# A hybrid decoder block on one core: the chunked scan spread over the projection steps, and the last attention head and last output parts in ascending order

## The chip, the core and the metric

The kernel runs on one NeuronCore of a Trainium2 chip. The metric is the device time of one execution in microseconds (us); the time of a kernel is the median over its runs. The engines are TensorE (PE, with its weight loads shown apart as PEld), VectorE (DVE), ScalarE (ACT), GpSimd (POOL) and SyncE (SP), which issues nearly all DMAs of this kernel in order from one queue.

## What is computed

One layer, 2048 tokens of width 1024, float32. The input is RMS-normalised and goes through one projection `w_in`, whose columns belong to three parallel branches; their outputs are joined to 2048 columns and go through one projection `w_out`:

```python
u = rms_norm(h, norm_g)
proj = einsum('bsd,de->bse', u, w_in)
q, k, v, z_att, f_raw, z_ssd, xbc, dt_raw, x_lru, z_lru = split(proj)
y_att = fox_attention(q, k, v, log_f, ...) * silu(z_att)     # 8 heads x 64, causal
y_ssd = ssd_mixer(xbc, dt_raw, z_ssd, ...)                   # 16 heads x 64, 2 groups, chunks of 128
y_lru = rglru_mixer(x_lru, ...) * silu(z_lru)                # 512 channels
h = h + einsum('bse,ed->bsd', concat([y_att, y_ssd, y_lru]), w_out)
```

The chunked scan (`ssd_mixer`) works for each chunk `c` of 128 tokens and each group `g` of 8 heads: a product C·B, weighted with the causal decay, times `x·dt` (the diagonal part); C times the carried state; and the new state, which is the old one decayed plus B times `x·dt·decay`. Its result is gated and its sum of squares kept for a group norm.

## The kernel before

All products are done in float32 split into a high and a low part (`float32r`, names ending in `h` and `l`), so that one projection is three products: high·high, high·low, low·high. The program is traced in Python; a scheduler then orders each engine's instructions from its own estimate of times, by priority (program order, unless a block raises it with `high_priority`), and adds the semaphores. Each engine runs its list in order. `issue_after(ins)` puts the instructions of a block that run on the engine of `ins` behind it.

The work comes in these stages, in the order of the program:

1. Norm and transposition of the input to `uh`, `ul` (four blocks of 512 tokens), projections of x/B/C with their convolution (`pxx`), the gates, v of heads 0 to 3, the LRU branch with its projections (`pll`, `pzl`) and the scan's gate z (`group_zs`, `pzs`), up to about 754 us. Intermediate results go to DRAM tensors (`xs_d`, `b_d`, `bt_d`, `ct_d`, `zs_d`, `acs_d`).
2. The scan: 16 chunks by 2 groups, 32 units of `ssd_unit`. A unit loads its tiles, makes `cb` (L675), twice loads a row of cumulated decays broadcast to all partitions into `ab` (L686), masks it on POOL (L689), takes exponentials on ScalarE (L693), multiplies by `cb` (L694) and makes four heads of `py` (L698). Then `po` from the state (L705), `pn` for the new one (L715), and the transposed result goes to `gt_d` (store, one unit late). The tile `ab` has two buffers.
3. Attention projections, traced behind the scan but with no dependence on it: for each head pair `p` eight calls of `proj_tok2` (`pqk`, L343 to L347), after p = 1 eight calls for v (`group_v`), after p = 2 and p = 3 eight calls each of `proj_ch` for the gate `z_att` (`group_za`, `pza`): 56 calls. Since the scan was traced first, the scheduler lets these calls fill in around it. After p = 2, `load_head(0)` and `load_q(0)` are traced. They load keys, values and queries of head 0 into tiles that lie where the scan's tiles lay.
4. Attention: `units` are (head, block of 256 queries), 64 of them, with `sb + 1` tasks each, 288 in all. `ORD` gives the order of the blocks: head 0 from block 7 down to 0, heads 1 to 6 up, head 7 down. Each task makes scores (`T`), two exponentials, and three tasks later the product with v (`O`); the row maxima for the next unit (`S`, L970) are spread over the tasks. `finish` closes a unit and calls `later(store, 1)`.
5. The output projection is a generator, `sweeps`, of 512 steps of three products (L1145 to L1147) each: 256 for the parts of LRU and scan group 1, then 256 for scan group 0 and attention (`work`). Four steps make a half of 512 columns in one PSUM bank, which VectorE then adds to `xr` or `xo` (L1151, L1153). During attention the pool `psP` has one bank; after it `psP2` has six. `fill` takes a number of steps after each attention task:

```python
want = FIRST + count[0] * RATE // 288 + MORE * max(0, count[0] - 288 + END)
```

A part of attention can be taken only when the head-7 unit that covers its tokens has been finished (`ready`); for that the row sums of all eight heads are read back from DRAM, inverted and written again (L1098 to L1100). `later(f, n)` runs `f` when the task counter has advanced by `n`. `work` runs through the tokens from the last tile to the first:

```python
work = [(NT - 1 - t, i) for t, i in work]
```

`anchor[1]` is the last product of the fifth of the last eight `pza` calls; the row maxima of the first attention unit and the first 12 output steps are put behind it.

## Time and profile before

| | us |
|---|---|
| median of 3 runs (2012.23 to 2016.85) | 2012.35 |
| profiled execution | 2011.36 |
| its span, first to last instruction | 2009.5 |
| TensorE busy | 1946.7 (97%) |
| TensorE weight loads busy | 1705.1 (85%) |
| VectorE busy | 1296.2 (65%) |
| ScalarE busy | 1005.0 (50%) |
| POOL busy | 807.9 (40%) |

The profiled execution is one run, on the slowest core; 1.86 us of its time lie outside the span. Busy times are shares over all stages. Matmuls are pipelined, so that the mean duration of one (400 ns for 512 columns) is longer than the distance from one to the next; what a product costs in a stream is read from a window, busy time by the number of records. The granted clock of TensorE is given as a share of 2.4 GHz; 0.50 is 1.2 GHz.

### The profile page before, as it was taken

What the parts mean: (1) busy time and instruction counts of PE and PEld (TensorE: products, weight loads), DVE (VectorE), ACT (ScalarE), POOL (GpSimd) and SP (SyncE); (2) the same over time, 40 slices, a digit from 0 to 9 for tenths busy, and PEclk for the clock granted to TensorE, in tenths of its full rate; (3) what the DMA queues carried; (4) which work ended last, traced back from release to release, by engine and by line L of the source; (5) the groups of instructions that cost most, each with busy time, mean ns of one, the idle gap of its engine ahead of it and who ended that gap; (6) DMA issues with size and microseconds to landing.
All of it is one profiled execution on the core that took longest, in us unless ns stands there. A gap on an engine that the chain in (4) does not pass through costs nothing.

```text
span 2009.5 us, 34885 instructions
## 1 busy us (share of the span) xinstructions
PE 1946.7 (97%) x11941; PEld 1705.1 (85%) x11941; DVE 1296.2 (65%) x2573; ACT 1005.0 (50%) x2174; POOL 807.9 (40%) x920
## 2 busy tenths in 40 slices
PE   7999999999999999899999999999999999998899
PEld 6898888898989899787888897888899888887787
DVE  6748555573645556767667534788788887896333
ACT  7625444453544544444444333576777776675010
POOL 0100000232222224445555200687888887786110
PEclk9999999999999999999999999999999999999999
DMA  5332223121212135657666724765565764523353
GB/s 191 84 100 67 70 74 105 48 65 43 70 38 75 32 114 140 185 169 209 206 198 175 197 81 141 217 166 156 164 169 163 196 161 143 173 83 113 123 173 126
DMA packets 260032, 261.30 MB, mean 130 GB/s; under 512 B 26724, under 2 KB 198016, under 8 KB 258304
## 3 DMA queue, kind: packets, MB, share of 16 engines
q1 hardware_dynamic: 259696, 259.05, 43.7%
q8 instruction: 95, 1.56, 0.3%
q0 software_dynamic: 160, 0.03, 0.1%
q14 instruction: 81, 0.66, 0.1%
HBM read 164.22 MB, written 94.77 MB: 129 GB/s over the span
## 4 chain that ended last, share of the span: by engine, by line
PE 44%; DMA 3%; DVE 2%; issue 1%; ACT 1%; POOL 1%; SPq 1%; DVEq 0%; POOLq 0%; ACTq 0%
PE po L1145 6%; PE po L1146 5%; PE po L1147 5%; PE T L1011 3%; PE T L1012 3%; PE O L1067 3%; PE O L1069 3%; PE S L970 3%; PE pza L360 1%; PE pza L361 1%; PE pza L359 1%; PE pqk L345 1%; PE pqk L343 1%; PE pqk L347 1%; DMA ab<-acs_d 1%
## 5 line engine op out<-in xcount | busy, mean ns | idle before, releaser
L1145 PE MATMUL po<-woh,mh 128*128 128x512 f32 x512 | 204.9, 400 | 13.9 <-DVE xo L1151 11.4
L1024 DVE TENSOR_TENSOR pl<-T,ph 128x512 fp32r<-128x512 f32 (+1 forms) x288 | 185.5, 652 | 38.9 <-ACT T L1023 32.7
L1146 PE MATMUL po<-wol,mh 128*128 128x512 f32 x512 | 202.4, 395 | 0.0
L1147 PE MATMUL po<-woh,ml 128*128 128x512 f32 x512 | 201.7, 395 | 0.0
L1022 ACT ACTIVATE ph<-T 128x512 fp32r<-128x512 f32 (+1 forms) x288 | 165.4, 574 | 51.0 <-PE T L1012 43.5
L1037 POOL TENSOR_TENSOR ac<-ac,ph 128x512 f32<-128x512 f32 x120 | 158.7, 1323 | 23.8 <-ACT ph L1022 18.1
L1023 ACT ACTIVATE T<-T 128x512 f32<-128x512 f32 (+1 forms) x288 | 164.7, 572 | 0.3
L359 PE MATMUL pxx<-uh,wh 128*128 128x512 f32 x384 | 152.8, 400 | 1.1 <-ACT uh L304 1.0
L360 PE MATMUL pxx<-ul,wh 128*128 128x512 f32 x384 | 153.1, 400 | 0.0
L361 PE MATMUL pxx<-uh,wl 128*128 128x512 f32 x384 | 150.9, 395 | 0.0
L347 PE MATMUL pqk<-wh,ul 128*128 128x256 f32 x512 | 150.9, 295 | 0.0
L980 DVE TENSOR_REDUCE mc<-S 128x1 f32<-128x512 f32 x192 | 128.5, 682 | 32.4 <-PE S L970 30.7
L1067 PE MATMUL O<-ph,vv 128*128 128x256 f32 (+1 forms) x576 | 148.1, 278 | 0.6 <-ACT ph L1022 0.5
L1011 PE MATMUL T<-q,k 128*128 128x256 f32 x576 | 146.3, 279 | 2.1 <-ACT q L995 1.6
L345 PE MATMUL pqk<-wl,uh 128*128 128x256 f32 x512 | 148.3, 290 | 0.0
L343 PE MATMUL pqk<-wh,uh 128*128 128x256 f32 x512 | 147.8, 289 | 0.0
L420 DVE SCALAR_TENSOR_TENSOR accx<-rtx,cv,accx 128x512 f32<-128x512 f32 x144 | 108.3, 753 | 57.7 <-ACT accx L417 54.7
L345 PE MATMUL pzs<-wl,uh 128*128 128x256 f32 x512 | 143.6, 281 | 0.0
L347 PE MATMUL pzs<-wh,ul 128*128 128x256 f32 x512 | 143.3, 281 | 0.0
L343 PE MATMUL pzs<-wh,uh 128*128 128x256 f32 x512 | 143.0, 281 | 0.0
L1012 PE MATMUL T<-qx,kx 128*128 128x256 f32 x576 | 142.7, 279 | 0.0
L1069 PE MATMUL O<-pl,vv 128*65 128x256 f32 x576 | 141.4, 277 | 0.0
(357 smaller groups left out, 5693.2 us busy)
## 6 DMA issues: line engine op xcount, KB each, us to landing
ab<-acs_d SPq DMA_DIRECT2D x64, 256.0 KB
pt_d<-xr SPq DMA_DIRECT2D x64, 256.0 KB
wr<-in_w_in_dram SPq DMA_DIRECT2D x112, 128.0 KB
xt<-in_x_dram SPq DMA_DIRECT2D x16, 512.0 KB
xs_d<-stx SPq DMA_DIRECT2D x32, 256.0 KB
v_d<-vs SPq DMA_DIRECT2D x32, 256.0 KB
wr<-in_w_in_dram SPq DMA_DIRECT2D x128, 64.0 KB
zs_d<-zs SPq DMA_DIRECT2D x32, 256.0 KB
```

The lines of the kernel that those rows point to most:

```text
L343: T.matmul(ps[:, i, :], h[k][:, sl], wh[k], start=(k == 0 and i == 0), stop=False, skip_group_check=True)
L345: T.matmul(ps[:, i, :], h[k][:, sl], wl[k], start=False, stop=False, skip_group_check=True)
L347: ins = T.matmul(ps[:, i, :], l[k][:, sl], wh[k], start=False, stop=last, skip_group_check=True)
L360: T.matmul(ps, wh[k][:, ms], ul[tb][k], start=False, stop=False)
L1011: T.matmul(ps, k2[:, ks], q3[:, qs], start=(jj == 0), stop=False, skip_group_check=True)
L1012: ins = T.matmul(ps, kx[:, ks], qx[:, qs], start=False, stop=True, skip_group_check=True)
L1024: marks["V"].append(V.tensor_tensor(pl[:, 0:n], pt[:, 0:n], ph[:, 0:n].bitcast(F32), op=ALU.subtract))
L1067: T.matmul(po[:, qs], vv[:, kt, 0:128], ph[:, cs], start=(kt == 0), stop=(kt == 2 * sb + 1), skip_group_check=True)
L1069: T.matmul(po[0:65, q2], vv[:, kt, 64:129], pl[:, cs], start=False, stop=False, skip_group_check=True)
L1145: T.matmul(ps, mh[:, j, :], h, start=(j == 0), stop=False)
L1146: T.matmul(ps, mh[:, j, :], l, start=False, stop=False)
L1147: T.matmul(ps, ml[:, j, :], h, start=False, stop=(j == 3))
```

## The change

The scan becomes a generator, `ssd_steps`. A unit yields after its loads, `cb` and the two `ab`; after `po`; after each half of `py`; and at its end: five times, 160 in all, with a last step for the closing norm. The calls of the attention projections now tick after every second `k`, four times a call. `scan` counts the ticks and takes scan steps such that 160 steps fall on `SPAN` = 184 of the 224 ticks. Each step is traced at raised priority, its TensorE instructions behind the projection product of the tick. `ab` gets a pool of four buffers. The store of a unit's result is split: transposition and copy at the end of the next unit, its DMA in the unit after that. While ticks run, the weights of the projections are traced at raised priority too. When the scan has ended, `begin` closes its pools, opens those of attention and loads head 0; this was traced after the scan and after p = 2 before.

Head 7 takes its blocks from 0 up to 7, `work` runs through the tokens from the first tile on, the term with `MORE` and `END` is removed from `fill`, and read-back, reciprocal and write of the row sums are called 2, 4 and 5 tasks after the unit's stores, its `ready` after 8. `run_late` takes the entries in the order of their due times.

```diff
-END = 14
-MORE = 2
-ORD = (DOWN,) + (UP,) * 6 + (DOWN,)
+ORD = (DOWN,) + (UP,) * 7
+SPAN = 184
...
+    def tick(ins):
+        if between[0] is not None:
+            between[0](ins)
...
+        if between[0] is not None:
+            with tc.high_priority(offset=HP):
+                return split_weights(cols, rawp, eng, i, n)
+        return split_weights(cols, rawp, eng, i, n)
...
+            if k % 2:
+                tick(ins)
...
+    s4 = sx.enter_context(tpool(name="s4", bufs=4, side="right"))
-    def ssd_unit(c, g):
+    def ssd_unit(c, g, before):
...
-        py = psY.tile([P, 512], F32, name=f"py{u}", tag="Y")
+        abs_ = []
         for q in range(2):
-            ab = s2.tile([P, 4, P], F32, name=f"ab{u}_{q}", tag="ab")
+            ab = s4.tile([P, 4, P], F32, name=f"ab{u}_{q}", tag="ab")
...
-            for e in range(4):
-                o = (q * 4 + e) * 64
-                T.matmul(py[:, o:o + 64], ab[:, e, :], xd[:, q * 4 + e, :], start=True, stop=True)
...
+            abs_.append(ab)
+        yield
+        last[1]()
         if state[g] is not None:
             po = psY.tile([P, 512], F32, name=f"po{u}", tag="Y")
...
+        yield
+        py = psY.tile([P, 512], F32, name=f"py{u}", tag="Y")
+        for q, ab in enumerate(abs_):
+            for e in range(4):
+                o = (q * 4 + e) * 64
+                T.matmul(py[:, o:o + 64], ab[:, e, :], xd[:, q * 4 + e, :], start=True, stop=True)
+            yield
...
+        before()
...
-            dma(gt_d[g][:, :, tsl].rearrange("i p t -> p i t"), yt)
...
+            last[1] = lambda: dma(gt_d[g][:, :, tsl].rearrange("i p t -> p i t"), yt)
+
+        last[0] = store
+
+    def ssd_steps():
+        for c in range(NT):
+            for g in range(2):
+                yield from ssd_unit(c, g, last[0])
+                yield
+        last[1]()
+        last[0]()
+        last[1]()
...
+    def begin():
...
+        make_k2(0)
+        load_head(0)
+        load_q(0)
...
+        def scan(ins):
+            done[0] += 1
+            while done[1] >= 0 and done[1] * SPAN < done[0] * 160:
+                done[1] += 1
+                with tc.high_priority(offset=HP), tc.issue_after(ins.ins):
+                    if next(ssd, 0) == 0:
+                        done[1] = -1
+                if done[1] < 0:
+                    begin()
+
+        between[0] = scan
...
-            if p == 2:
-                load_head(0)
-                load_q(0)
+        between[0] = None
...
-            dma(sr, s_d[qt].rearrange("i h t -> (i h) t"))
-            V.reciprocal(sr, sr)
-            dma(r_d[qt].rearrange("i h t -> (i h) t"), sr)
-            later(lambda: ready.add(sb), 4)
+            later(lambda: dma(sr, s_d[qt].rearrange("i h t -> (i h) t")), 2)
+            later(lambda: V.reciprocal(sr, sr), 4)
+            later(lambda: dma(r_d[qt].rearrange("i h t -> (i h) t"), sr), 5)
+            later(lambda: ready.add(sb), 8)
...
-        while late and (t is None or late[0][0] <= t):
-            late.pop(0)[1]()
+        while True:
+            due = [z for z in late if t is None or z[0] <= t]
+            if not due:
+                return
+            due = min(due, key=lambda z: z[0])
+            late.remove(due)
+            due[1]()
...
-        work = [(NT - 1 - t, i) for t, i in work]
...
-        want = FIRST + count[0] * RATE // 288 + MORE * max(0, count[0] - 288 + END)
+        want = FIRST + count[0] * RATE // 288
```

## Rows read from the trace of the kernel before

**Rows 1.** Cores: span of each and mean granted clock of TensorE.

```profile
core 0: 2009.5 us, clock 0.993
```

**Rows 2.** Windows by stage: us, busy us (instructions) of five engines, granted clock, DMA share, GB/s.

```profile
754.00:1123.00 369.00, 345.34 (x2487) 304.71 (x2486) 254.31 (x430) 171.67 (x483) 179.52 (x181) 0.98 0.62 181
...
1253.00:1300.00 47.00, 43.98 (x242) 37.01 (x240) 32.52 (x71) 23.04 (x48) 30.23 (x27) 0.96 0.77 217
1300.00:1800.00 500.00, 495.06 (x3268) 444.34 (x3267) 417.72 (x989) 365.44 (x836) 408.46 (x453) 1.00 0.55 157
1800.00:1850.00 50.00, 44.01 (x288) 39.31 (x287) 35.90 (x84) 32.83 (x76) 36.51 (x43) 1.00 0.40 119
1850.00:1900.00 50.00, 40.75 (x159) 31.52 (x159) 17.34 (x37) 4.76 (x9) 6.65 (x8) 0.90 0.38 118
1900.00:2000.00 100.00, 100.00 (x443) 82.81 (x442) 41.46 (x94) 11.20 (x18) 10.34 (x8) 1.00 0.49 156
2000.00:2009.50 9.50, 5.68 (x26) 4.36 (x24) 2.26 (x6) 0.00 (x0) 0.00 (x0) 0.92 0.25 96
```

**Rows 3.** Windows, finer, around the end of attention; columns as above.

```profile
1750.00:1800.00 50.00, 49.10 (x315) 42.78 (x315) 46.78 (x98) 35.57 (x79) 40.70 (x38) 1.00 0.29 99
...
1850.00:1855.00 5.00, 2.18 (x12) 1.52 (x11) 1.33 (x3) 1.04 (x3) 2.08 (x4) 0.94 0.61 189
1855.00:1860.00 5.00, 3.73 (x9) 2.99 (x10) 2.42 (x5) 0.00 (x0) 0.72 (x1) 0.50 0.19 56
```

**Rows 4.** Waits of TensorE, 750 to 1130 us: sum, times, longest us.

```profile
PE py L698 <- DVE ab L694: 6.7, 6, 1.9
PE py L698 <- issue: 3.1, 3, 1.5
PE py L698 <- POOL xs L701: 2.6, 1, 2.6
```

**Rows 5.** Chain that ended last, in the scan: start, us, what.

```profile
1088.28 4.58 DMA ab<-acs_d
1092.98 0.65 POOL ab L689
1093.65 1.29 ACT ab L693 x4
1095.02 0.70 DVE ab L694
1095.76 1.24 PE py L698 x8
```

**Rows 6.** Waits of the DMA queue SP, 750 to 1260 us.

```profile
SPq L686 <- PE py L698: 50.8, 34, 3.1
```

**Rows 7.** Waits of TensorE, 1800 to 1900 us.

```profile
PE po L1145 <- DVE xo L1151: 11.4, 5, 3.7
```

**Rows 8.** Waits of VectorE, 1780 to 1900 us.

```profile
DVE sr L1099 <- DMA sr<-s_d: 10.3, 4, 4.5
```

**Rows 9.** Windows of `pqk` alone: us, TensorE busy (records), clock, DMA share, GB/s.

```profile
1150.00:1200.00 50.00, 40.10 (x332) 1.00 0.32 92
```

**Rows 10.** Windows of `pza` alone; columns as in the group above.

```profile
1200.00:1250.00 50.00, 42.46 (x179) 1.00 0.43 140
```

**Rows 11.** Timeline of SP: start us, us of issue, instruction.

```profile
1136.78 0.46 SPq L805 DMA_DIRECT2D k<-kh_d  x1
...
1148.41 0.46 SPq L822 DMA_DIRECT2D qx<-ql_d  x1
...
1233.42 15.90 SPq L405 DMA_DIRECT2D za_d<-zt  x4
```

**Rows 12.** Timeline of POOL; in brackets idle time before and its releaser.

```profile
1136.99 0.52 POOL L778 MEMSET q<- 64x512 f32 x1 [7.44 <-DMA gt_d<-yt]
```

**Rows 13.** Line L698: records, duration ns, first and last start us.

```profile
L698 PE MATMUL py<-xd,ab x512: 217/275/446, 762.3 to 1123.2; 128*128 128x64 f32 x171
```

**Rows 14.** Line L970; columns as above.

```profile
L970 PEld LDWEIGHTS S<-k,q x320: 186/188/286, 1235.6 to 1826.4; 96*128 96x128 f32 x160
```

More of the change, by code (lines that the diff above doesn't have):

```diff
@@ L178, in hybrid_block @@
                    for k in range(KD)])
+    anchor = [None, None]
+    between = [None]
+    def tick(ins):
+        if between[0] is not None:
+            between[0](ins)
     gcount = [0]
@@ L361, in proj_ch @@
             ins = T.matmul(ps, wl[k][:, ms], uh[tb][k], start=False, stop=(k == KD - 1))
+            if k % 2:
+                tick(ins)
         anchor[0] = ins
@@ L783, in hybrid_block @@
-    for i in range(2):
-        make_q(kc)
-    k2s = {}
-    def make_k2(b):
-        k2 = (kvB if b else kvA).tile([P, S], F32R, name=f"k2{b}")
-        G.memset(k2[64:128, :].bitcast(F32), 0.0)
-        G.memset(k2[96:97, :].bitcast(F32), -1.0)
-        k2s[b] = k2
-    make_k2(0)
+    kp_ = {}
     heads = {}
     qs_ = {}
+    q3s, qxs = [], []
+    k2s = {}
     def load_head(h):
@@ L823, in load_q, with make_q, make_k2 @@
         qs_[j // 2] = q3, qx
+    kc = kvA = kvB = zm = onr = idr = zmt = None
+    def make_q(pool):
+        i = len(q3s)
+        q3 = pool.tile([P, 512], F32R, name=f"q3{i}")
+        G.memset(q3[64:128, :].bitcast(F32), 0.0)
+        G.memset(q3[64:66, :].bitcast(F32), 1.0)
+        q3s.append(q3)
+        qxs.append(pool.tile([P, 512], F32R, name=f"qx{i}"))
+    def make_k2(b):
+        k2 = (kvB if b else kvA).tile([P, S], F32R, name=f"k2{b}")
+        G.memset(k2[64:128, :].bitcast(F32), 0.0)
+        G.memset(k2[96:97, :].bitcast(F32), -1.0)
+        k2s[b] = k2
+    def begin():
+        nonlocal kc, kvA, zm, onr, idr, zmt
+        sx.close()
+        sgx.close()
+        kc = cx.enter_context(tpool(name="kc", bufs=1, side="right"))
+        kvA = cx.enter_context(tpool(name="kvA", bufs=1, side="right"))
+        zm = kc.tile([P, 640], F32, name="zm")
+        G.memset(zm, 0.0)
+        G.affine_select(out=zm[:, 512:640], in_=zm[:, 512:640], pattern=[[-1, P]],
+                        compare_op=ALU.is_ge, fill=-NEG, base=0, channel_multiplier=1)
+        onr = kc.tile([P, 65], F32R, name="onr")
+        G.memset(onr[:, 0:64].bitcast(F32), 0.0)
+        G.memset(onr[:, 64:65].bitcast(F32), 1.0)
+        idr = kc.tile([P, P], F32R, name="idr")
+        V.tensor_copy(idr, ident)
+        zmt = kc.tile([P, P], F32R, name="zmt")
+        V.tensor_scalar(zmt, tri, NEG, -NEG, op0=ALU.mult, op1=ALU.add)
+        for i in range(2):
+            make_q(kc)
+        make_k2(0)
+        load_head(0)
+        load_q(0)
     def load_wo(ws, k0, half, last, behind=()):
```

56 lines of the change are left out of this document (14 added, 42 removed).

## The prediction

> **What bounds the kernel now.** I read the span first [rows 1], then the span cut into stages [rows 2]. The reader is to see that TensorE is the bound from end to end: in the output stretch 1900 to 2000 us it is busy all 100 us, in the attention loop 1300 to 1800 it sits idle 500 − 495.06 = 4.94 us, 1%. No other engine comes near; the busiest, VectorE, has 417.72 of 500 there. So the time can only shrink where TensorE is idle or runs below its full clock, and the stages show two such places.
>
> The first is 754 to 1123 us, where the scan runs beside the q/k projections: 369 − 345.34 = 23.7 us idle, and a granted clock of 0.98 where the loop and the output stretch have 1.00. The second is the end of attention, 1800 to 1900: 5.99 + 9.25 = 15.2 us idle, and 0.90 of the clock in its second half, as the 5 us from 1855 at 0.50 show [rows 3]: the lower of the two levels, 1.2 GHz. In the 5 us ahead of that the engine had been busy for 2.18 only.
>
> Then the waits inside these places. In the scan TensorE waits before the diagonal product `py` (L698): 6.7 us for the multiplied decay tile `ab` (L694), 3.1 us where the profile names no releaser, 2.6 us for POOL [rows 4]. The chain shows why: decay row by DMA 4.58, mask 0.65, four exponentials 1.29, product with `cb` 0.70, then `py` 1.24 [rows 5]: 8.5 us in a row, and the DMA can only start when a buffer of `ab` is free. There are two; SP waited 50.8 us, 34 times, for `py` to free one [rows 6]. A unit took (1123 − 754)/32 = 11.5 us, so this chain plus the product sets the scan's pace. At the end of attention TensorE waits 11.4 us in 5 waits for VectorE's eviction L1151 [rows 7]: output halves pass through one PSUM bank (`psP`), and each has to be evicted before the next starts. VectorE itself waits 10.3 us in four waits for the sums' read-back `sr` (L1098) with evictions queued behind the reciprocal [rows 8].
>
> **Part A, the scan in steps.** No product is added or removed. What changes: the 161 scan steps are tied to 185 of the 224 marks (`tick`, four to a call) of 56 projection calls, `ab` has four buffers, and the products `py` stand two steps behind the `ab` work. How long is a step? A q/k or v call has 48 products of 256 columns; p = 3 shows 40.10/332 = 0.121 us each [rows 9], 5.8 us a call. A gate call has 24 products of 512 columns at 42.46/179 = 0.237 [rows 10], 5.7 us. So a mark is 1.44 us of projection, and a step takes 185/161 = 1.15 marks, 1.65 us, plus the scan's own products. 46 calls are 266 us; the scan's products and the q/k transposes fill the rest of the stage. The stage from 754 to 1253 has 499 − 23.7 = 475 us of TensorE work, the last 9¾ calls are 56 of it, so the scan spreads over about 420 us, 13 us a unit. `ab` now has two steps (about 5 us) between its product with `cb` and `py`, and its DMA may start up to two units ahead, so the 8.5 us chain is covered. What covers the scan's VectorE, ScalarE and POOL work is the same as now, spread thinner (254, 172 and 180 us of 369 today).
>
> What can be gained: the 23.7 us idle, and the clock. (1 − 0.98) × 369 = 7.4 us of clock time; part of it fell on idle time, so I bound it between 0 and 7 and take 4. Bound above: 31; below: nothing, if the waits only move. How much stays? The nearest row is the attention loop, where other work is already hung behind named products in this way: 1% idle, here 4.7 us of 470. I take 28 − 5 = **23 us**.
>
> The edits around it: the raw weights and their casts get priority inside this stretch so that the scan's do not pass them; no instruction is added. The unit's store issue moves one step later, off SP's queue while the copy is unfinished. Both at nothing, covered by the projections; without that cover the weights would cost a fraction of one group's first cast.
>
> **Part B, head 0's load.** `begin()` now runs at mark 185, after the scan's last unit, instead of the load being traced after p = 2's gate group. Before, the head's loads really left at 1136.8 us, and the last part at 1148.4 [rows 11], since POOL's memset waited 7.44 us for the last scan store [rows 12]. The last `py` started at 1123.2 [rows 13]; so the loads begin 13.6 us behind the scan and are complete some 30 us behind it (estimate: issue end 25 us plus a few us landing). First use `S` was at 1235.6 [rows 14], 110 us behind the scan. After the change the scan ends about 60 us before the stage's end and `S` is tied to the fifth of the last eight gate calls, some 20 us before it: 40 us, still above 30. Bounds: 0, or, if SP is held as in its 15.9 us of `za_d` stores [rows 11], about 10 us of waiting. I take **1 us lost**.
>
> **Part C, the last head and the output parts.** With the largest unit first, the last head ended on units of one to three steps; each ends with stores, a read-back, a reciprocal and a write, all close together: the 10.3 us on VectorE [rows 8] and SP's waits behind them. In the new order the small units come right after head 6 and its largest last, as at every other head boundary; these lie in 1300 to 1800 at 1% idle. The read-back, reciprocal and write are now called 2, 4 and 5 steps after the stores, when their inputs should have landed. `MORE` had asked for 2 × 14 = 28 extra output steps of 3 products at the end; without it 12 + 290 = 302 of 512 are called inside attention. Behind 1850 us the trace has 159 + 443 + 26 = 628 products [rows 2], 209 steps, so 303 were done: the extra ones were not run in time, they stood in line for one bank. Removing them moves no work. Taking tokens from the first on, the tail reads partial sums written long before.
>
> Gain: 15.2 us idle plus clock (0.10 × 50 = 5 us, part of it in idle time: 3), 18 us. What stays: the change from attention to pure output needs new PSUM banks, as at attention's start, where 47 − 43.98 = 3.0 us were idle [rows 2], plus the 0.9 of the window 1750 to 1800 [rows 3] and a unit's closing sums; I take 5.5. Bounds 0 to 20, taken **12.5**.
>
> **Sum.** The profiled execution took 2011.36 us, 1.86 outside its span; the median is 2012.35, 1 us above. 2011.4 − 23 + 1 − 12.5 = **1977 us**.
>
> **Rivals.**
> Waits move only: in the fixed order a `py` or `po` placed behind a named product still finds its input late, because real durations differ from planned ones. For it: today's order had a plan too, and 12.4 us of these waits [rows 4]. Against: two steps of distance. Then A gives nothing: 2011.4 + 1 − 12.5 = 2000; with part of C lost too, 2007.
>
> Head 0 late: SP's queue holds the loads, 10 us lost instead of 1: 1986.
>
> The end gains nothing, since the last unit's read-back now stands alone in front of the output stream: 1989.5.
>
> Slower: TensorE takes its products in order. Each unit puts six scan groups between projection products; if VectorE, in order too, waits in `yo` or `st` for a late scan product, the evictions of q/k behind it are late, three PSUM banks fill, and projections stop as well. Today a unit loses 23.7/32 = 0.74 us. At that loss the time is the first rival's 2000; each 0.1 us more costs 3.2, so it decides from 0.74 + 11/32 = 1.1 us a unit, and at 1.5 us the time is about 2025. The Trainium skill (TensorE: Matmul & The Clock Gate, "Part 2: What happens when you issue a matmul") says that the products stay in program order and only weight loads are pulled ahead; by that rule a scan product that is not ready stops every projection product behind it, which is this rival. The trace agrees that one late operand idles the whole engine [rows 4], but not that it is often late.
>
> **How the numbers follow.** Forecast 0.60 (its own range 1966 to 1988); waits only move 0.13; head late 0.10; end gains nothing 0.07; slower 0.10. Changes within 0.3% (6 us) can't be told from none. Faster: 0.60 + 0.10 + 0.07 + 0.05 of the first rival = 0.82; same: its other 0.08; slower 0.10. The range 1962 to 2001 leaves out the slower rival, half the first one's tail and a little on the fast side. The best case is 2011 − 31 − 20 = 1960.
>
> **What would show it.** After: idle TensorE of the projection stretch under 10 us with clock 1.00; `py` spread to about 1165 us; SP's waits for `py` at L686 nearly gone; `S` first at about 1210 without a wait; the wait at L1145 for L1151 and at L1099 for `sr` down to a few us; about 209 output steps behind attention. Wrong if `py`, `po` or `S` carry waits of more than 10 us in sum, if VectorE shows waits for scan products, or if the last unit's read-back holds the first output parts.

## The result, and the profile after

The changed kernel takes 1997.22 us (median of 6 runs, 1995.6 to 2005.07) against 2012.29 of the kernel before in the same comparison (6 runs). The ratio is 0.9938, 95% interval 0.9922 to 0.9954, about 12.5 us (9 to 16). So it is faster, as forecast, and inside the range; but 1977 was forecast, so the gain is little over a third of the 34 us expected.

The profiled execution is the slowest of its six runs, 2005.07 us. A stage's length therefore says more here than the total. I cut the span at three products: the last `z` product of the scan (`pzs`), the first and the last score product of attention (`T`). "Projections" lie between the first two, "attention" between the last two, "the end" behind; idle is a stage's length less TensorE's busy time.

| stage | before: us (idle) | after: us (idle) |
|---|---|---|
| projections | 508.6 (26.2) | 498.5 (22.4) |
| attention | 584.6 | 594.3 |
| the end | 162.2 | 151.8 |

The projections as a whole, before and after, and then the windows of the kernel after, columns as in [rows 2]:

```profile
754.10:1262.70 508.60, 482.44 (x3282) 423.90 (x3280) 311.85 (x565) 212.67 (x569) 192.19 (x201) 0.98 0.59 171
758.80:1257.30 498.50, 476.11 (x3282) 419.74 (x3280) 301.17 (x566) 210.56 (x562) 186.81 (x199) 0.99 0.59 173
```

```profile
756.00:1256.00 500.00, 478.04 (x3301) 422.10 (x3301) 301.58 (x567) 210.46 (x562) 186.81 (x199) 0.99 0.59 173
1300.00:1500.00 200.00, 197.47 (x1309) 177.38 (x1308) 164.32 (x407) 146.63 (x342) 162.39 (x190) 1.00 0.59 165
1500.00:1600.00 100.00, 96.01 (x618) 85.62 (x616) 77.55 (x182) 68.06 (x154) 78.33 (x86) 0.97 0.65 189
1600.00:1800.00 200.00, 196.94 (x1291) 175.83 (x1291) 169.89 (x397) 146.13 (x336) 163.08 (x181) 1.00 0.49 135
1800.00:1850.00 50.00, 43.92 (x273) 38.22 (x272) 38.91 (x78) 30.74 (x67) 34.08 (x35) 0.97 0.31 91
1850.00:1900.00 50.00, 47.77 (x214) 39.37 (x214) 21.24 (x46) 6.96 (x14) 11.52 (x11) 0.97 0.49 149
```

Four things are to be seen. The projections still idle 22 us. Most of the 10.1 us by which they are shorter is busy time, 482.44 to 476.11, with the same products; the granted clock rose from 0.98 to 0.99. The 50 us behind 1850 idle 2.23 where they idled 9.25 [rows 2], and the end is 10 us shorter. And there is a new hole: 1500 to 1600 idles 4 us at clock 0.97, in a loop that ran at 1% idle.

**What took the place of the waits at `py`.** TensorE's waits of the kernel after in the projections, columns as in [rows 4]:

```profile
PE po L718 <- DVE st L748: 6.5, 5, 2.5
PE ptq L944 <- DVE stl L951: 6.4, 6, 1.4
PE ptq L944 <- DVE qk L939: 2.2, 3, 0.8
PE pza L372 <- ACT wh L209: 2.1, 1, 2.1
PE S L1017 <- DVE mc L1027: 2.0, 2, 1.6
...
PE py L727 <- DVE ab L711: 0.5, 1, 0.5
```

The 6.7 us of `py` for `ab` [rows 4] are 0.5. All waits of `py` in the stage were 17.1 us and are 1.0. In their place stand waits of `po`, hardly any before and 6.6 now, of `ptq`, 2.3 before and 8.7 now, and of `pza`, hardly any before and 2.1 now. SP still waits for `py` as often as in [rows 6]:

```profile
SPq L703 <- PE py L727: 50.2, 32, 4.1
```

One of the five waits of `po`, first on VectorE, then on TensorE (timelines: start us, us, instruction, in brackets the idle time before it and its releaser):

```profile
1054.94 0.69 DVE L735 TENSOR_TENSOR y<-y,zz 128x512 f32<-128x512 f32 x1
1059.15 1.25 DVE L210 TENSOR_TENSOR wl<-wr,wh 128x256 fp32r<-128x256 f32 x1 [3.52 <-ACT wh L209]
1060.32 0.68 DVE L748 TENSOR_TENSOR st<-st,pn 128x512 f32<-128x512 f32 x1
```

```profile
1054.49 0.59 PE L740 MATMUL pn<-xe,bm 128*128 128x512 f32 x1
...
1055.28 0.36 PE L356 MATMUL pqk<-wh,uh 128*128 128x256 f32 x1
...
1058.30 0.28 PE L360 MATMUL pqk<-wh,ul 128*128 128x256 f32 x1
1061.05 1.12 PE L718 MATMUL po<-st,ct 128*128 128x512 f32 x2 [2.47 <-DVE st L748]
1061.61 0.80 PE L372 MATMUL pza<-uh,wh 128*128 128x512 f32 x1
```

The next unit's `po` needs a bank of `psY`, of which there are three for five tiles a unit; the one in turn holds this unit's `pn` until `st` has read it. `st` stands in VectorE's list behind a weight's low part `wl`, which waits 3.52 us for ACT's cast. So `po` waits 2.47 us and the gate products `pza` stand behind it. The change itself brought `po` nearer: its diff puts `po` in front of `py`, where it stood behind it. In the kernel before, at the same place:

```profile
1052.52 0.59 PE L715 MATMUL pn<-xe,bm 128*128 128x512 f32 x1
...
1058.70 1.89 PE L698 MATMUL py<-xd,ab 128*128 128x64 f32 x16
1060.43 1.08 PE L705 MATMUL po<-st,ct 128*128 128x512 f32 x2
```

Over 30 units the median time from the end of `pn` to the next unit's first `po`, without the wait in front of `po`, was 8.1 us before and is 4.0 after. Before, the tile that took the bank of `pn` was the next unit's `py`, at a median of 5.9 us. The wait of `po` is the mechanism of the "slower" rival, in small. The Trainium skill (TensorE: Matmul & The Clock Gate, "Part 2: What happens when you issue a matmul") says that products stay in program order; by these rows the trace agrees.

**The new hole in attention.** Around 1574 us TensorE waits once for ACT (first fence), since ACT waits for the store of an earlier row of sums (second); the third shows why on SP (start us, us of issue):

```profile
PE T L1058 <- ACT q L1042: 3.5, 1, 3.5
```

```profile
ACT su L1129 <- DMA s_d<-su: 4.2, 1, 4.2
```

```profile
1546.30 0.42 SPq L1275 DMA_DIRECT2D xo<-pt_d  x1
...
1555.32 0.59 SPq L796 DMA_DIRECT2D k<-kh_d  x1
...
1558.26 7.99 SPq L1251 DMA_DIRECT2D pt_d<-xr  x1
...
1568.79 0.60 SPq L1139 DMA_DIRECT2D s_d<-su  x1
```

Behind a head's loads SP's next issue is held for 8 us, and the store of the sums stands behind it. What holds it the trace doesn't show. The hold is there at other heads too; new are three loads of output tiles `xo`, 512 KB each, at 1515.72, 1534.65 and 1546.30, some 200 us before their use. They may leave so early because, with the tokens taken from the first on, the partial sums that they read have long been written.

### The profile page after: what moved, and what is told of

It is laid out like the page before. It is cut to its first block, busy times and chain, and to the rows that moved or that the text cites. A ratio compares the mean times of both kernels' runs of the same rounds, so it can differ in the third digit from the quotient of the medians.

```text
span 2003.4 us, 34852 instructions
## 1 busy us (share of the span) xinstructions
PE 1945.2 (97%) x11941; PEld 1705.6 (85%) x11941; DVE 1287.7 (64%) x2573; ACT 1004.3 (50%) x2174; POOL 804.5 (40%) x920
## 4 chain that ended last, share of the span: by engine, by line
PE 82%; DMA 6%; DVE 6%; ACT 3%; issue 2%; POOL 1%; SPq 1%; DVEq 0%; POOLq 0%; ACTq 0%
PE po L1192 6%; PE po L1194 5%; PE po L1193 5%; PE pxx L372 4%; PE pxx L373 4%; PE pxx L374 4%; PE pzs L358 3%; PE pzs L356 3%; PE pzs L360 3%; PE T L1058 3%; PE T L1059 3%; PE S L1017 3%; PE O L1114 3%; PE O L1116 3%; PE py L727 2%
## 5 line engine op out<-in xcount | busy, mean ns | idle before, releaser
L1069 ACT ACTIVATE ph<-T 128x512 fp32r<-128x512 f32 (+1 forms) x288 | 165.4, 574 | 55.9 <-PE T L1059 48.1
L1084 POOL TENSOR_TENSOR ac<-ac,ph 128x512 f32<-128x512 f32 x120 | 157.6, 1313 | 22.5 <-ACT ph L1069 17.6
L356 PE MATMUL pqk<-wh,uh 128*128 128x256 f32 x512 | 155.3, 304 | 0.0
L710 ACT ACTIVATE ab<-ab,nacs 128x128 f32<-128x128 f32 x256 | 82.8, 392 | 125.6 <-POOL ab L706 125.2
L360 PE MATMUL pqk<-wh,ul 128*128 128x256 f32 x512 | 144.2, 282 | 0.0
```

Source lines behind the costliest of these rows:

```text
L356: T.matmul(ps[:, i, :], h[k][:, sl], wh[k], start=(k == 0 and i == 0), stop=False, skip_group_check=True)
L360: ins = T.matmul(ps[:, i, :], l[k][:, sl], wh[k], start=False, stop=last, skip_group_check=True)
```

## The experiments

Medians, ratios to the kernel before in the same comparison with their intervals, and the stages of the profiled execution. "Idle at the end" is TensorE's idle time from 100 us before the last `T` to 50 us behind it.

| kernel | median us | ratio | projections (idle) | attention | idle at the end |
|---|---|---|---|---|---|
| before | 2012.3 | | 508.6 (26.2) | 584.6 | 16.1 |
| after | 1997.2 | 0.9938 [0.9922, 0.9954] | 498.5 (22.4) | 594.3 | 9.9 |
| e1 scan only | 2001.2 | 0.9954 [0.9932, 0.9976] | 498.4 (22.6) | 583.3 | 15.7 |
| e2 end only | 2008.3 | 0.9982 [0.9967, 0.9997] | 502.9 (22.6) | 590.8 | 8.9 |
| e3 low parts on POOL | 2000.9 | 0.9942 [0.9924, 0.9959] | 494.9 (21.9) | 593.3 | 9.2 |
| e4 load after weights | 2000.0 | 0.9938 [0.9917, 0.9959] | 495.7 (19.9) | 593.0 | 9.2 |
| e5 `xo` late | 1992.3 | 0.9906 [0.9873, 0.9938] | 493.6 (21.3) | 586.5 | 8.4 |
| e6 tokens from the last | 2009.3 | 0.9984 [0.9961, 1.0007] | 494.7 (19.6) | 569.5 | 23.4 |
| e7 four banks | 2014.9 | 1.0023 [1.0006, 1.0040] | 500.4 (23.9) | 594.0 | 9.6 |
| e8 weights plain | 1999.8 | 0.9949 [0.9931, 0.9967] | 499.7 (23.8) | 594.5 | 9.7 |
| e9 no scan (one run) | 1845.6 | | 345.0 (5.5) | 592.1 | 9.3 |
| e10 two `ab` | 2001.7 | 0.9955 [0.9938, 0.9972] | 496.0 (22.6) | 595.1 | 8.4 |
| e11 scan over 36 calls | 2001.0 | 0.9951 [0.9934, 0.9968] | 496.4 (18.6) | 595.1 | 10.2 |
| e12 e5 and e3 | 1993.3 | 0.9924 [0.9902, 0.9946] | 495.4 (20.5) | 587.6 | 9.0 |
| e13 y on POOL | 2001.8 | 0.9963 [0.9944, 0.9983] | 506.8 (28.8) | 587.6 | 8.7 |
| e14 xs, xe on VectorE | 1984.1 | 0.9870 [0.9838, 0.9903] | 487.5 (14.5) | 587.1 | 9.1 |
| e15 state on VectorE | 1996.8 | 0.9925 [0.9897, 0.9952] | 500.6 (22.5) | 587.2 | 9.2 |
| e16 all four on VectorE | 1984.2 | 0.9866 [0.9844, 0.9889] | 486.4 (13.1) | 587.9 | 10.3 |
| e17 before, xs and xe on VectorE | 2006.6 | 0.9980 [0.9967, 0.9993] | 505.1 (19.4) | 582.9 | 16.1 |
| e18 e14 and e3 | 1991.8 | 0.9904 [0.9885, 0.9923] | 496.8 (20.2) | 587.2 | 9.0 |

The comparisons were made at different times, and in the later ones the median of the kernel before is 2010.4 to 2012.0; medians of two rows are compared across them, so a few us between rows say little.

In the projections, before and e2 run the same instructions in the same order on TensorE, VectorE, ScalarE and POOL, and so do after, e1, e5 and e6 (but for one instruction of POOL in e6). Their differences are what executions vary by: 508.6 and 502.9 us with 26.2 and 22.6 idle for the first two, 493.6 to 498.5 us with 19.6 to 22.6 idle for the other four. So smaller differences of that stage are not read alone. On the means, the steps shorten the stage by 9.4 us; 2.9 of it is idle time, 6.5 busy time.

### The parts alone: e1 and e2

e1 is the changed kernel with the end of before (order of the last head, `MORE`, tokens from the last on, read-backs in place); e2 is the kernel before with only the end changed.

```diff
# e1: against the changed kernel
-ORD = (DOWN,) + (UP,) * 7
+ORD = (DOWN,) + (UP,) * 6 + (DOWN,)
...
+        work = [(NT - 1 - t, i) for t, i in work]
```

> The changed kernel with the last head, the order of the output parts, MORE and the calls of the row sums as before; only the scan is spread. If the two parts add (theory), the stretch from the last pzs product to the first S keeps the 491 us of the changed kernel (501 before), the end keeps the 15 us idle of before, and the time is about 10 us under before, ratio 0.994 to 0.997. If the scan part gains nothing and all comes from the end (rival), the time is that of before within 4 us.

> The kernel before with the last head ascending, output parts from the first tokens, no MORE and the row sums' steps called apart; the scan as before. If the parts add (theory), about 7 us under before, ratio 0.995 to 0.998, with about 9 us idle of TensorE in the last stretch of attention. Rival: the end's gain shows only together with the spread scan, then within 3 us of before.

The scan alone brings 0.46%, 9.3 us, the end alone 0.18%, 3.6 us. The sum, 12.9, agrees with the whole change's 12.5; the intervals leave 3 to 4 us either way on each. The hole near 1574 us is in e2 too and not in e1: it belongs to the end's edits. At the end e1 still has before's waits [rows 7] (`po` for `xo` 11.2 us in 5 waits), e2 has none.

### The scan's waits, first guesses: e3, e4, e7, e8, e10, e11

```diff
# e3: low parts of the weights on POOL inside the projections
-                return split_weights(cols, rawp, eng, i, n)
+                return split_weights(cols, rawp, (G,), i, n)
# e4: begin() once the last weights are asked for
-                if done[1] < 0:
-                    begin()
+            if done[1] == -1 and done[0] > 192:
+                begin()
+                done[1] = -2
# e7: PSUM banks
-    psY = pb.enter_context(tpool(name="psY", bufs=3, space=PSUM))
-    psj = pb.enter_context(tpool(name="psj", bufs=3, space=PSUM))
+    psY = pb.enter_context(tpool(name="psY", bufs=4, space=PSUM))
+    psj = pb.enter_context(tpool(name="psj", bufs=2, space=PSUM))
# e8: no raised priority for the weights
-            with tc.high_priority(offset=HP):
-                return split_weights(cols, rawp, eng, i, n)
# e10
-    s4 = sx.enter_context(tpool(name="s4", bufs=4, side="right"))
+    s4 = sx.enter_context(tpool(name="s4", bufs=2, side="right"))
# e11
-SPAN = 184
+SPAN = 144
```

> The changed kernel with the low parts of the q, k, v and gate weights made on POOL instead of VectorE. Theory: VectorE runs its list in order, and a low part that waits for its cast holds the scan's state update behind it, so that po waits. Then the 6.5 us of waits of po for st fall under 2 us and the stretch from the last pzs product to the first S goes from 491 to 485 to 488 us, ratio to before 0.990 to 0.993. Rival: the three banks of psY alone make po wait; then these waits stay above 5 us and the time is that of the changed kernel.

> The changed kernel with begin, and so head 0's load, called eight marks later, when the weights of the last gate group have been traced. Theory: head 0's load stands in SP's queue in front of these weights; then the 2.1 us wait of pza for its cast goes, the clock stays 1.00 there, and the stretch from the last pzs product to the first S is 2 to 4 us shorter, unless S now waits for its keys. Rival: the weights are late for another reason, or S waits as long as pza did; then no change within 1 us, or up to 5 us slower.

> The changed kernel with one more PSUM bank for the scan's products (`psY` 4 instead of 3) and one less for the projections (`psj` 2 instead of 3). Theory (`po` waits because its bank is that of the unit before's `pn`, which VectorE empties late behind the weights' low parts): the five waits of `po` for `st`, 6.5 us, go; the stretch from 756 to 1256 us loses up to 6 us of idle unless the projections, with two banks, wait in their place. Rival (VectorE's list is late as a whole, and the bank is only where it shows): the same 20 to 22 us of idle come back as waits of the projections' products for their own evictions (ptq, pqk, pza), and the stage stays at 495 to 499 us.

> The changed kernel without the raised priority on the weights' loads and casts inside the projections: they are planned by the scheduler like any other work. Theory (the raised weights' low parts stand in VectorE's list ahead of scan evictions and wait there for ACT's cast, which holds everything behind them): the waits of `po` for `st` (6.5 us) shrink, VectorE's waits for ACT's cast (23.5 us) shrink, and the stage is up to 6 us shorter. Rival (without it the scan's work stands in front of the casts): TensorE's projections wait for the weights, pqk and pza for `wh` or `wl`, by more than 6 us, and the stage is longer than 500 us. As forecast, the edit is worth nothing: the stage stays at 495 to 499 us.

> The changed kernel with two buffers of the decay tile `ab`, as before, instead of four; the steps stay. A unit uses two, so with four the next unit's can be loaded while this one's are in use, and with two they can't. Theory (the two steps between `ab` and `py` alone don't cover the load of 4.6 us, mask, exponentials and product; the buffers do): `py` waits for `ab` again, several us in sum, and the stage is 4 to 10 us longer than the changed kernel's 494 to 499. Rival (distance in steps is what counts): the waits of `py` stay under 2 us in sum and the time within 0.3% of the changed kernel's.

> The changed kernel with the same scan steps over about 36 calls (SPAN 144) instead of 46, so a unit has about 10 us of projections instead of 13. Theory (VectorE is the engine that is late, and its load sets how much TensorE idles: less time for the same evictions and products means more waits): the stretch with the scan idles more than the 16 to 18 us it does now, and what idles behind 1180 us (the waits of pza and ptq, 4 us) goes, so the time is 0 to 8 us above the changed kernel's. Rival (idle belongs to places in the projections where weights change, not to the scan's pace): the idle of the stage falls by those 4 us and the time is 3 to 5 us below.

None of the six moved the time from the changed kernel's by more than its runs scatter, but e7, which lost: idle stayed between 18.6 and 24 us, and which waits hold it differed. In e7 the waits of `po` are gone as expected, and others came:

```profile
PE pza L372 <- ACT wh L209: 5.9, 1, 5.9
PE ptq L944 <- DVE stl L951: 3.9, 4, 1.4
PE py L727 <- POOL st L746: 3.2, 2, 2.0
PE py L727 <- POOL xs L731: 2.7, 3, 1.3
```

So one more bank for the scan didn't take the idle time away. Whether the bank is only where the lateness shows e7 can't tell, since the same edit took a bank from the projections, which alone cost some 11 us of idle ahead of the scan, 24.4 instead of 13.5. In e8 `po` waits 6.4 us as before the edit: the raised priority shows no worth, as forecast. In e10 `py` waits 1.6 us for `ab`, 3.6 in all, and the stage is no longer: the steps more than the buffers took the waits at `py` away. In e11 the idle time is 4 us lower, as its rival said, but only 1 us under what the changed kernel's own order varies by, and the median didn't follow. e4 did not confirm that head 0's loads hold back the last gate weights (`pza` still waits 2.6 us for the cast).

### The hole in attention: e5 and e6

```diff
# e5: the load of an output tile stays behind the last load of the second part
-                loads.append(dma(xs[t], pt_d[tsl, :]))
+                put = dma(xs[t], pt_d[tsl, :])
+                if loads:
+                    tc.add_manual_dep(put.ins, loads[-1].ins.name, mybir.DependencyInfo(
+                        mybir.DependencyClass.NoSync, mybir.DependencyReason.DATA))
+                loads.append(put)
# e6: tokens from the last to the first, as before
+        work = [(NT - 1 - t, i) for t, i in work]
```

> The changed kernel, with one edge added: the loads of the output tiles `xo` (512 KB each) are tied behind the last load of the second output part, so that on SP the first three stand where the token order from last to first had put them, and no other engine's list differs. Theory (the token order from first to last lets three `xo` loads be planned 200 us early, right ahead of a head's load; together they hold SP and the store of the row sums behind them, and ACT, then TensorE wait at about 1574 us): the wait of T for ACT near 1574 us is gone, attention's TensorE idle falls from 8.5 us to about 4.6, from the wait near 1451 to the one near 1617 us it takes 158.6 us instead of 165, the time is 4 to 6 us below the changed kernel's, about 1992 to 1995. Rival (the wait belongs to the head's own load or to the new plan of the row sums): the stretch stays at 162 to 165 us and the time at that of the changed kernel.

> The changed kernel, with one line of before put back: the output parts take their tokens from the last to the first again. The rest of the change at the end (last head from the smallest unit, later read-backs, no extra output steps) stays. Theory (the token order does two things: it moves the `xo` loads early, which costs about 5 us near 1574, and it spares the end the wait for partial sums just written, which is worth little): the wait near 1574 us is gone, the end's idle stays near 10 us, and the time is 3 to 6 us below the changed kernel's. Rival A (the end's gain of 6 to 7 us comes from the token order itself): the end's idle is back at 15 us, and the time equals the changed kernel's within 2 us. Rival B (the wait near 1574 belongs to other parts of the change): it stays.

e5 moves the three issues on SP, and two others by a place or two; the lists of the other four engines are those of the kernel after. The hole is gone: its window, then its hold on SP.

```profile
1500.00:1600.00 100.00, 99.48 (x653) 89.23 (x652) 82.27 (x193) 71.15 (x161) 82.24 (x90) 1.00 0.59 170
```

```profile
1542.21 0.59 SPq L796 DMA_DIRECT2D k<-kh_d  x1
...
1545.15 7.73 SPq L1251 DMA_DIRECT2D pt_d<-xr  x1
```

The hold is still there, 7.73 us. But e5 started attention 1257.3 − 1248.4 = 8.9 us earlier, so on the time axis of the kernel after its hold begins at 1554.1 instead of 1558.26: the early `xo` loads had pushed SP's list 4.2 us late, which is ACT's wait of 4.2. From the small wait of `S` at 1442.60 to that of `O` at 1601.20 e5 takes 158.6 us, the kernel after 165.4 (1451.44 to 1616.84). Attention is 7.8 us shorter, and 586.5 to 587.9 us in every kernel below that has e5's edge, against 590.8 to 595.1 in those that have the end's edits and the early loads. The theory holds; the rival is out. The median is 4.9 us lower, but the intervals of the two ratios overlap, so that size is rough.

e6 takes the hole away too (158.7 us for that stretch), but its end lost far more:

```profile
PE po L1192 <- ACT mh L1171: 13.2, 1, 13.2
PE O L1124 <- ACT ah L1095: 5.1, 1, 5.1
```

With the last tokens first, the first last-part product needs the unit that ends last. So my theory for e6 fell, and rival A was right and too mild: the ascending order of the last head and that of the tokens belong together. (The token order alone, with the last head as before, was not run.)

### Is it the scan at all: e9

```diff
+        yt = s1.tile([P, 4, P], F32, name="yt", tag="yt")
...
-                yield from ssd_unit(c, g, last[0])
+                for i in range(4):
+                    yield
+                dma(gt_d[g][:, :, c * P:(c + 1) * P].rearrange("i p t -> p i t"), yt)
...
```

> The changed kernel with the scan left out of the projections: its 161 steps only store constants into the 32 places where the scan's result would go, so what is computed behind it is not the reference's. It measures what the projections of 756 to 1256 us idle by themselves. Theory (the idle time belongs to the scan: its evictions and the projections' stand in one VectorE list, and whichever is late holds the other): the idle of the stretch falls from 22 us to under 7, with no wait of ptq and pza above 1 us each. Rival (the projections' own stores, casts and transposes make half of it): idle stays above 11 us, with the waits of ptq for `stl` (6 us) and of pza for the cast `wh` (2 us) still there.

```profile
756.00:1100.00 344.00, 338.91 (x2455) 318.83 (x2455) 139.23 (x345) 102.77 (x223) 7.69 (x13) 0.99 0.45 136
```

```profile
PE ptq L945 <- DVE stl L952: 2.6, 1, 2.6
PE S L1018 <- DVE mc L1028: 2.4, 3, 1.6
```

Without the scan the projections idle 5.5 us, two of which stand at the first `S`. So about 17 of the 22 us come with the scan, as the theory said; and the scan costs TensorE 476.1 − 339.5 = 137 us of its own products (busy time of the stage with and without it).

### Which engine is late: e13 to e18

All but e17 start from e5, so its 493.6 us of projections and 21.3 idle are the point to compare with.

```diff
# e13
-            V.tensor_tensor(y, y, yo, op=ALU.add)
-        V.tensor_tensor(y2, y2, zz, op=ALU.mult)
+            G.tensor_tensor(y, y, yo, op=ALU.add)
+        G.tensor_tensor(y2, y2, zz, op=ALU.mult)
# e14 (e17: the same on the kernel before)
-        G.tensor_tensor(xs, xs, drow[:, hs] ...
+        V.tensor_tensor(xs, xs, drow[:, hs] ...
-            G.tensor_tensor(xe, xs, dec[ ...
+            V.tensor_tensor(xe, xs, dec[ ...
# e15 (e16: this, xd and both of e14)
-                G.tensor_tensor(st, st, etot[ ...
+                V.tensor_tensor(st, st, etot[ ...
```

> The kernel of e5 (the first `xo` loads late), with two of the scan's VectorE instructions of each unit, y + yo (0.81 us) and y * zz (0.87 us), on POOL, 52 us of VectorE's 302 in the stretch. The reference point is e5: projections 493.6 us, idle 21.3, waits of po for `st` 6.7 and of ptq for `stl` about 6. Theory (TensorE idles because VectorE works its list in order and is late with evictions that stand behind the scan's y chain): the waits for `st`, `stl` and `cb` shrink, idle falls by 5 us or more, projections under 490, time about 1987. Rival (the evictions wait for ACT's casts and for stores, not for VectorE's work): idle stays at 20 to 23 us, and POOL, which had 187 us, may make py wait for its mask and products.

> The kernel of e5, with two of the scan's POOL products of each unit on VectorE instead: xs times drow (1.10 us on POOL) and xs times dec (1.14 us), some 62 instructions, about 50 us more of VectorE at its 0.8 us each. Theory (VectorE's list is what TensorE waits for): idle of the projection stage rises from 21.3 by 5 us or more, in waits for VectorE's evictions, and the time is 5 to 10 us above e5's 1992. Rival (VectorE's load isn't what is late): idle and time stay within 3 us of e5's.

Both theory and rival fell. Less work on VectorE made the stage 13 us longer, more work on it 6 us shorter. Against the mean of the four executions of e5's order, 496.3 us, these are 10.5 and 8.8, and the single runs do not overlap: e14 takes 1982.1 to 1986.7 us, e5 1988.8 to 1996.6, e13 2000.4 to 2007.4. The stretch from 756 to 1256 us in e5, e13, e14 and e16:

```profile
756.00:1256.00 500.00, 478.64 (x3322) 423.61 (x3321) 307.57 (x576) 215.28 (x572) 191.91 (x204) 1.00 0.58 175
```

```profile
756.00:1256.00 500.00, 472.08 (x3251) 417.15 (x3249) 264.85 (x495) 209.87 (x557) 251.36 (x258) 0.98 0.57 169
```

```profile
756.00:1256.00 500.00, 485.52 (x3361) 430.00 (x3360) 339.17 (x646) 217.32 (x578) 136.78 (x147) 0.99 0.60 178
```

```profile
756.00:1256.00 500.00, 486.89 (x3369) 432.04 (x3368) 360.60 (x707) 216.26 (x577) 68.90 (x88) 0.99 0.61 179
```

The third and the fifth busy time are to be read: VectorE rises from 264.85 (e13) over 307.57 (e5) to 339.17 and 360.60 while TensorE idles less. So VectorE's amount of work is not what is late. New theory: POOL's products, which stand in order behind its wait for the decay row.

> The kernel of e5, with one POOL product of each unit on VectorE: the state times its decay (1.07 us on POOL, 28 to 30 times), which VectorE's `st` add waits for and which stands on POOL behind xe and xs. New theory (POOL is in order; its second mask waits for the decay row's load, 76 us in sum, and everything of the unit behind it, xe, xs and the state, is late, which holds `st`, the bank of `pn` and so the next `po`): the waits of po for `st` (6.7 us in e5) fall under 3, idle of the projection stage falls from 21.3 by 3 us or more, time 1986 to 1990. Rival (what e14 gained came from xs and xe, on the way to y and pn, and the state is never the last): idle stays at 20 to 23 us and the time at 1990 to 1996.

> The kernel of e14, with the other two POOL products of each unit on VectorE too, x times dt and the state times its decay, so POOL has only the masks; VectorE has some 45 us more. Theory (POOL's order is what is late): idle falls under e14's 14.5 us, or stays there if nothing on POOL is late any more; time 1978 to 1985. Rival (from here on VectorE's amount of work is what is late): idle rises above 18 us, time above 1988.

> The kernel before, with xs times drow and xs times dec on VectorE instead of POOL, and nothing else. It shows whether what e14 found is a property of the scan or of the steps. Theory (the products on POOL are late in either order): the time falls by 4 to 10 us, 2001 to 2007. Rival (in the old order the chain from the decay row to py sets the pace, and it has no POOL product in it but the mask): within 3 us of 2011.

> The kernel of e14 with the weights' low parts made on POOL inside the projections, where POOL now has 137 us of 500. Theory (VectorE's list has the waits for ACT's cast in front of scan evictions, 20 us in sum, and POOL has room): idle of the projection stage under 12 us, time 1979 to 1984. Rival (POOL in order now holds the masks behind a wait for the cast): idle above 16 us, time above 1986.

The state's product is not it (e15: idle 22.5, rival right). Moving all four gains no more than xs and xe (e16: 13.1 idle, 1984.2 us, at the top of its expected range). In the kernel before the same two products bring 0.20% [0.07, 0.33], 4 us, where e14 brings some 8 over e5: a part of the gain is in the scan and not in the steps. And e18 gives back what e14 gained, as its rival said: POOL now waits for the cast, its wait in the projections:

```profile
POOL wl L210 <- ACT wh L209: 32.8, 21, 9.4
```

So in e13, e14, e16 and e18 less work on POOL goes with less idle time. That POOL's order is the cause is argued and not shown, and three things of the record stand against taking it so. The edit of e18 put on the changed kernel and on e5 (e3 and e12) cost nothing that shows, although POOL waits for the cast there too (18.9 and 19.4 us). The state's product, taken off POOL alone, gained nothing (e15). And moving an instruction made the scheduler plan all lists anew: in the projections some 200 of TensorE's 3280 instructions stand elsewhere in e14 than in e5, and no run held the other lists fixed. What e14 took away is not the wait shown above either: `po` waits 5.5 us in the stage (e5: 6.8) and 7.8 in e16; it is `ptq`, 3.9 (7.7), and `pza`, 1.2 (2.7).

Why xs and xe, is not settled: in e5's timeline xs is done well before `y` reads it (1141.31 + 1.04 against 1148.79 us), so it isn't plainly the last input, and neither product was moved alone. POOL's products also have a second price, and it is a rival. These are y · zz on VectorE in e5, e14 and e16, and on POOL in e13 (groups: busy us, mean ns):

```profile
L735 DVE TENSOR_TENSOR y<-y,zz 128x512 f32<-128x512 f32 x32 | 27.7, 867 | 0.6
```

```profile
L735 DVE TENSOR_TENSOR y<-y,zz 128x512 f32<-128x512 f32 x32 | 25.9, 808 | 0.5
```

```profile
L735 POOL TENSOR_TENSOR y<-y,zz 128x512 f32<-128x512 f32 x31 | 41.1, 1327 | 0.0
```

The same for `qk` times its norm, the product that each `ptq` transposes, in e13, e5, e14 and e16:

```profile
L939 DVE TENSOR_TENSOR qk<-qk,rqk 128x512 f32<-128x512 f32 x32 | 30.8, 1019 | 0.2
L939 DVE TENSOR_TENSOR qk<-qk,rqk 128x512 f32<-128x512 f32 x32 | 25.6, 859 | 0.2
L939 DVE TENSOR_TENSOR qk<-qk,rqk 128x512 f32<-128x512 f32 x32 | 22.4, 757 | 0.1
L939 DVE TENSOR_TENSOR qk<-qk,rqk 128x512 f32<-128x512 f32 x32 | 21.8, 738 | 0.1
```

The instruction y · zz takes 867 ns beside four POOL products a unit, 808 beside two, 761 beside none (e16), and 1327 on POOL itself; the medians on VectorE are 708, 691 and 686, so the difference is a few long ones, up to 1.5 us in e5 and e14 and 1.1 in e16. (In the kernels before and after, also beside four, the mean is 1039 and 897.) `y` from `py` and xs (L732), whose one input lies in PSUM, takes 686 to 688 in all of them. And xs, 1102 ns on POOL, takes 723 on VectorE. The Trainium skill (Perfetto Trace Analysis, "Optimizing Scalar/DVE Operations") warns that the two engines share a read port, so that moving work between them might not help; these means agree with the sharing, and moving work to VectorE helped. So VectorE's own products, made longer by POOL's, could be what is late: over e13, e5, e15, e14 and e16 the mean of `qk` (1019, 859, 871, 757, 738 ns) goes with the idle time (28.8, 21.3, 22.5, 14.5, 13.1 us). But e10, e12 and e18 have it at 774, 770 and 721 with 22.6, 20.5 and 20.2 idle. No run separates this from POOL's order or from the new plan.

**The version that beats both** is e14: 1984.06 us, 0.9870 of before, 13 us below the changed kernel; e16 is as fast.

### Two edits together: e12

> The changed kernel with two of the edits of this study: the first `xo` loads tied behind the last load of the second output part, and the weights' low parts made on POOL inside the projections. The first took the wait near 1574 us away (attention 586.5 instead of 594.3 us), the second left the projections at 494.9 instead of 498.5. Theory (both are causes and add up): 5 to 9 us below the changed kernel, 1988 to 1992. Rival (only the loads count, and the stage's 3.6 us are what a run varies by): 4 to 6 us below, 1992 to 1994, with the projections at 494 to 499.

1993.3 us, with the projections at 495.4: the rival was right. Only the late loads count; what e3 seemed to save in the stage is what executions differ by.

## Why the prediction was right in direction and wrong in size

**Part A** failed at the sentence "the nearest row is the attention loop ... I take 28 − 5 = 23". Measured: 9.3 us (e1). The clock's 4 us in that 28 came about right: the stage's clock of 0.983 before and 0.990 after stands for 8.5 and 5.1 us. The idle time is what failed: 23.7 − 5 = 19 us of it were to go, and between the executions of the old and the new order 2.9 us are gone. The other 6.5 us are busy time; the clock can make up some 4 of them, and what the rest is, is not shown. The chain from `ab` to `py` was read rightly: of the 12.4 us of waits that it explains [rows 4] about one is left, and of all 17.1 us of `py` 1.0. But the 23.7 us of idle time were all credited to it, and a later stage's idle share was taken for what would stay. The step put distance in front of `py` and took it from `po`: placed ahead of `py`, `po` follows `pn` after 4.0 us of products instead of 8.1, and it was late next, with `ptq` and `pza`. The prediction doesn't weigh this; what would be late next was answered with a borrowed 1% and not looked for in the unit. That the shorter distance is why `po` waits is argued: no run put `po` back behind `py`. And why `ptq` waits longer stays open; e14 shows only that the place of xs and xe bears on it.

The first rival ("waits move only", 0.13) named what happened to the idle time; that its 2000 us is 3 from the measured time is half luck, for A gave 9 us that it denied and C 9 less than it granted. The slower rival named the engine at which the waits show, VectorE with its evictions in order, though e14 shows that the amount of VectorE's work does not set them.

Two smaller steps of A were wrong without costing anything: SP's waits for `py` did not go (50.2 us, [rows 6] 50.8), since four `ab` buffers are one unit ahead and not two; and e10 gives no sign that they were needed. "The edits around it ... at nothing" held for the weights (e8); the store's later issue was not run alone.

**Part B** was right: `S` starts at 1230.5 with the same 2.0 us of waits for `mc` as before, nothing lost. It is 20 us later than the 1210 forecast because the scan kept its stalls (last `py` 1180.4, forecast 1165).

**Part C** was right in its mechanism and off in two terms. The waits for `xo` of [rows 7] are gone and the idle time at the end fell from 16.1 to 8.4–9.9 us; I had left 5.5. Alone the end brings 3.6 us (e2). Without the hole e5 shows roughly what it is worth: 2001.2 (e1) − 1992.3 (e5) = 8.9 us instead of 12.5. The step that failed is "taking tokens from the first on, the tail reads partial sums written long before": right, and its other side was not asked. What is ready early can be loaded early, and three loads went 200 us ahead, into the queue in front of a head's load, at 4.9 us. The read-backs, called later, are still waited for on VectorE (8.5 us, [rows 8] 10.3), but with the small units earlier no wait of TensorE there names them. That removing the extra steps moves no work held: behind the last `T` stand 624 products of the output, 208 steps, before and after. (Of the 628 records that the prediction counted, six are attention's and five stand in two windows.)

In sum: 9.3 + 8.9 − 4.9 = 13.3, measured 12.5, where 23 + 12.5 − 1 = 34.5 was forecast. The 8.9 and the 4.9 share the median of e5, so only their difference, 4.0, is tested by this sum.

## What to carry to other kernels

When a stall is taken out of a fixed order, write down the distance of every other pair of producer and consumer in the same unit, before and after the edit: moving one product away from its input moves another nearer to its own, and another loop's idle share is no estimate of what stays. When data is made ready earlier, ask which DMA may now leave earlier, and what stands behind it on its queue: one edge that holds it back was worth some 5 us here. Which engine is late is not read from the releaser's name in the list of waits: VectorE was named nearly everywhere, and two runs that moved work in opposite directions showed that its amount of work is not it. And run one order twice before a difference of a stage is read: here the same lists differed by 6 us.

## What was not expected of the hardware

After eight issues of a head's loads near 1550 us SP's next issue lasted 7.43 us in the kernel before, 7.99 after and 7.73 in e5, with early `xo` loads or without; what it waits for is not shown. A product of 128 x 512 floats took 1.05 to 1.33 us on POOL and 0.68 to 1.04 on VectorE (means of a line), and y · zz on VectorE got faster by 12% (867 to 761 ns from e5 to e16) as POOL's products left. And the scan's products, which looked small beside the projections, hold TensorE for 137 us.
